# A conv and RWKV-7 block on one core: the last LayerNorm in the first phase, x loaded ahead in the second, BK times KR in quarters, squared keys summed in two products

## The chip, the cores and the metric

The kernel runs on one core of one Trainium2 chip. The core has TensorE (PE, matrix products, into the eight banks of PSUM), VectorE (DVE), ScalarE (ACT), GpSimd (POOL) and SyncE (SP); the last issues every DMA of this kernel, in the order in which they stand in its queue, and 16 DMA engines carry them between HBM and SBUF. The engines run each its own instruction stream and wait for each other on semaphores. The metric is device microseconds for one execution, less is better.

## The reference, cut to what matters

```python
D_MODEL = 1024; SEQ = 2048; CONV_WIDTH = 31; RWKV_HEAD = 64          # one batch, one layer
h = _rmsnorm(x, norm_g) * (1.0 + scale) + shift
p = h @ w_in                                                          # 1024 -> 9344
c_val, c_gate, c_og, ts, r_og, g_conv, g_rwkv = split(p)
# convolution branch
u = c_val * sigmoid(c_gate)
u = causal_depthwise_conv(u, conv_k, conv_b)                          # width 31
u = layernorm(u, ln_g, ln_b); y_conv = (silu(u) * silu(c_og)) @ w_conv_out
# RWKV-7 branch
r, k, v, w_low, a_low = split(token_shift(ts, mu))
decay = exp(-exp(-softplus(-(w0 + tanh(w_low) @ w2)) - 0.5)); a = sigmoid(a0 + a_low @ a2)
kk = k * k_k; kk = kk / max(sqrt(sum(kk * kk, per head)), 1e-12)
k = k * (1 + (a - 1) * k_a)
state = state * decay - (state @ kk) (kk * a)^T + v k^T;  o = state @ r   # a scan over time
o = layernorm(o, per head); o = (o + sum(r * k * r_k) * v) * silu(r_og); y_rwkv = o @ w_rwkv_out
# merge
m = sigmoid(g_conv) * y_conv + sigmoid(g_rwkv) * y_rwkv
out = _rmsnorm(x + gate * (m @ w_out), final_g)
```

All data are fp32.

## The kernel before

The 2048 positions are four blocks `b` of 512 (`TB`), the 1024 channels eight tiles of 128; features lie on partitions, time along the free axis. Each large product is made of three fp32r products: weights and activations are split into a rounded part `hi` and a remainder `lo` (an ACT cast and a DVE or POOL subtraction), and `mm3k` issues hi·hi, hi·lo and lo·hi into one PSUM bank. A projection of one weight tile is 24 such matmuls.

**First phase.** For each block, four groups `g` of four heads (two channel tiles, "pairs") are worked. The projections of `w_in` run all the time; between them stand, in bursts, the small products of the RWKV scan. `pair` prepares decay and keys of two heads: squared keys `sq` go through `bones` (a matrix of ones in two blocks of 64) to give each head's sum, which is copied (`ssr`) and sent by DMA (`dN`) to the place where the inversion of the group reads it; then BK times KR gives the 64 by 64 matrices within a chunk, two heads `hh` on the two halves of the rows. `group` inverts them (31 steps on POOL) and runs the chain over the eight chunks. `conv` makes u, and `taps` the 31 taps of its channel tile as 31 DVE operations; three u tiles exist. The result goes to `y_dram`. `lnorm_first(b)` is the LayerNorm of the conv branch for blocks 0 to 2, on POOL for the most part: it loads y three times (sum, squared differences, result), writes `u_dram`, and takes its tiles from a ring of seven, `hx`. The LayerNorm of block 3 is `lnorm(3)` in the second phase. `presplit` splits the output weights ahead of time and stores both parts.

After block 3, the output products `ro` and `co` of block 0 run (`rows0`).

**What sets the order.** The first phase is written by a planner. Generators (`Task`, by rank) yield conditions on planned times; `note` plans each instruction's time from a table of costs, and `poll` lets tasks issue while the projections go on matmul by matmul. `order` gives the sequence of projections in a group: three of k, r, v for each pair, and the fillings of the table `FILL`, for the last group `LAST` ("c" is a convolution, "1" to "4" the four gates). On the engines the order is then fixed. The second phase is ordered by the compiler's own scheduler.

**Second phase.** For each block: the conv output product (`cproj`, not for block 0), z and u of the next block loaded and split (`lsplit`), x loaded into `xt`, the output projection in four column blocks `cb` (PSUM tiles `pout`, 96 matmuls each), `addx` (adding x, and squares for the norm), `finish` (scale and store), then `rproj` for the next block, whose results `mr` use the buffers of `xt`. For block 0 `pout` uses the two banks that the projections use too. The program records nearly all instructions through one helper, so most lines of the profile read L129.

## Time and profile before

| | |
|---|---|
| median of 3 runs | 2893.17 us (2893.12 to 2894.62) |
| the profiled execution | 2892.82 us, its span 2890.7 us |
| mean granted TensorE clock | 0.982 |
| DMA | 680.47 MB, 235 GB/s, 69.0% of 16 engines' span |

The page cuts the span into 40 slices; a digit is the busy share of a slice in tenths:

```profile
PE   6999999889999999999999999999999998899998
DVE  6877787869677878885868787669787666543343
POOL 0564746533528355444656462648373633100000
DMA  8786767666757566776756686866666848676665
```

A slice is 72 us; the second phase begins in slice 34, at about 2397 us, where PE shows two 8s. In a row of groups, `out<-in` names the tiles, then come size and count, the busy time, the mean of one in ns, and after the second bar the idle time of the engine before them with what ended it. A matmul in fp32 leaves two records, one in fp32r leaves one; matmuls are pipelined, so a record's length is more than the time by which it holds the engine up, which is read from the distance of two starts.

### The profile page before, as it was taken

The numbers are of one execution on the slowest core, as the hardware profiler recorded it, in microseconds if no ns is written. First come the engines' busy times: TensorE is split into PE (matmuls) and PEld (weight loads), VectorE is DVE, ScalarE is ACT, GpSimd is POOL, SyncE is SP. The second block draws the span as 40 slices with busy tenths as digits, with TensorE's granted clock in tenths as the row PEclk, the third lists the DMA queues.
The fourth block names the chain that finished last, engine by engine and source line by source line (L and its number), as shares of the span: only waits on it lengthen the run. The fifth ranks groups of instructions, "written<-read, shape, count | busy, mean of one in ns | idle before, by whom it ended". The sixth has DMA issues, their size and how long they took to land.

```text
span 2890.7 us, 52304 instructions
## 1 busy us (share of the span) xinstructions
PE 2725.4 (94%) x19472; PEld 2201.6 (76%) x19472; DVE 2058.8 (71%) x3575; ACT 1090.7 (38%) x2180; POOL 1257.7 (44%) x1772
## 2 busy tenths in 40 slices
PE   6999999889999999999999999999999998899998
PEld 5777777667777777787777777777777777698988
DVE  6877787869677878885868787669787666543343
ACT  5545344434243434443434443333434233221211
POOL 0564746533528355444656462648373633100000
PEclk9999999989999999999999999999999999999999
DMA  8786767666757566776756686866666848676665
GB/s 329 255 295 219 281 221 263 237 227 234 231 187 257 183 218 237 250 258 221 252 181 233 205 294 201 273 211 215 205 246 213 294 158 314 234 240 229 215 226 175
DMA packets 361742, 680.47 MB, mean 235 GB/s; under 512 B 134160, under 2 KB 152912, under 8 KB 361488
## 3 DMA queue, kind: packets, MB, share of 16 engines
q1 hardware_dynamic: 361488, 677.13, 69.0%
q8 instruction: 154, 2.52, 0.4%
q14 instruction: 100, 0.82, 0.1%
HBM read 494.34 MB, written 181.54 MB: 234 GB/s over the span
## 4 chain that ended last, share of the span: by engine, by line
PE 32%; DVE 9%; POOL 7%; DMA 5%; issue 3%; ACT 1%; SPq 1%; DVEq 0%; POOLq 0%; ACTq 0%
PE ps_main L129 21%; PE pout L129 5%; DVE acc L129 3%; PE xo L129 2%; PE aux L129 2%; POOL TT L129 2%; POOL itmp L129 1%; PE late L129 1%; SPq L129 1%; DVE S L129 1%; DMA w_lo<-kl_in 1%; POOL oc L129 1%; DVE gst L129 1%; DVE rs_t L129 1%; POOL lny L129 1%
## 5 line engine op out<-in xcount | busy, mean ns | idle before, releaser
L129 PE MATMUL ps_main<-h_hi,w_hi 128*128 128x512 f32 x2432 | 1016.7, 418 | 17.4 <-DVE lora L129 4.6
L129 PE MATMUL ps_main<-h_hi,w_lo 128*128 128x512 f32 x2432 | 967.7, 398 | 20.3 <-POOL w_lo L129 13.6
L129 PE MATMUL ps_main<-h_lo,w_hi 128*128 128x512 f32 x2432 | 963.8, 396 | 2.0 <-DVE h_lo L129 2.0
L129 DVE SCALAR_TENSOR_TENSOR acc<-u,ck,acc 128x512 f32<-128x512 f32 x928 | 697.5, 752 | 25.3
L129 PEld LDWEIGHTS ps_main<-h_hi,w_lo 128*128 128x128 f32 x2432 | 463.4, 191 | 130.7 <-POOL w_lo L129 16.8
L129 PEld LDWEIGHTS ps_main<-h_hi,w_hi 128*128 128x128 f32 x2432 | 464.0, 191 | 128.9 <-issue 10.0
L129 PEld LDWEIGHTS ps_main<-h_lo,w_hi 128*128 128x128 f32 x2432 | 464.9, 191 | 99.8 <-issue 7.8
L129 POOL TENSOR_TENSOR w_lo<-w_st,w_hi 128x1024 fp32r<-128x1024 f32 (+1 forms) x83 | 165.2, 1990 | 302.9 <-ACT w_hi L129 248.7
L129 POOL TENSOR_TENSOR TT<-TT,itmp 128x126 f32<-128x126 f32 (+22 forms) x496 | 207.3, 418 | 38.9
L129 ACT ACTIVATE th<-ps_main 128x512 f32<-128x512 f32 x160 | 95.6, 598 | 333.9 <-PE ps_main L129 281.7
L129 ACT CAST w_hi<-w_st 128x1024 fp32r<-128x1024 f32 (+1 forms) x135 | 127.2, 943 | 243.2 <-DMA w_st<-w_co_t 137.3
L129 POOL TENSOR_TENSOR itmp<-La,TT 128x126 f32<-128x126 f32 (+22 forms) x496 | 200.8, 405 | 37.1 <-issue 6.4
L129 DVE SCALAR_TENSOR_TENSOR S<-xo,pe,Se 64x64 f32<-64x64 f32 x512 | 145.0, 283 | 90.1 <-PE xo L129 65.3
L129 ACT COPY uv<-xo 64x256 f32<-64x256 f32 (+1 forms) x192 | 81.0, 438 | 238.3 <-PE xo L129 164.7
L129 POOL TENSOR_TENSOR lny<-lny 128x512 f32<-128x512 f32 x90 | 119.9, 1340 | 108.9 <-DMA lny<-y_d 87.0
L129 DVE TENSOR_TENSOR w_lo<-w_st,w_hi 128x1024 fp32r<-128x1024 f32 x52 | 72.4, 1392 | 68.3 <-PE ps_main L129 46.5
L129 ACT ACTIVATE Se<-S,pe 128x128 f32<-128x128 f32 x256 | 88.7, 396 | 83.2 <-DVE S L129 82.7
L129 DVE TENSOR_TENSOR As<-aux,maskA 128x512 f32<-128x512 f32 x128 | 82.3, 685 | 52.5 <-PE aux L129 52.5
L129 POOL TENSOR_TENSOR wlo<-wf,wl 64x128 fp32r<-64x128 f32 x64 | 31.2, 488 | 149.6 <-ACT wl L129 147.0
L129 ACT ACTIVATE t<-ps_main,mu 128x512 f32<-128x512 f32 x96 | 65.9, 687 | 77.6 <-PE ps_main L129 68.0
L129 DVE TENSOR_TENSOR xt<-pout,xt 128x256 f32<-128x256 f32 x64 | 24.4, 419 | 99.3 <-PE pout L129 93.2
L129 PEld LDWEIGHTS xo<-S,KR 128*128 128x128 f32 x512 | 76.8, 189 | 23.9 <-DVE S L129 5.3
(298 smaller groups left out, 5029.0 us busy)
## 6 DMA issues: line engine op xcount, KB each, us to landing
w_hi<-kh_in SPq DMA_DIRECT2D x219, 512.0 KB
w_lo<-kl_in SPq DMA_DIRECT2D x219, 512.0 KB
w_st<-w_in_t SPq DMA_DIRECT2D x73, 512.0 KB
kh_in<-w_hi SPq DMA_DIRECT2D x71, 512.0 KB
kl_in<-w_lo SPq DMA_DIRECT2D x71, 512.0 KB
lny<-y_d SPq DMA_DIRECT2D x72, 256.0 KB
w_hi<-kh_ro SPq DMA_DIRECT2D x32, 512.0 KB
w_lo<-kl_ro SPq DMA_DIRECT2D x32, 512.0 KB
```

The lines of the kernel that those rows point to most:

```text
L129: r = f(*a, **k)
```

## The change

Four things change together.

1. `pair`: `sq` is split into `sq_hi` and `sq_lo`, and two fp32r products with `bones` take the place of one in fp32.
2. `pair`: each product of BK and KR is cut into two column halves of BK; in turn come the two heads' first halves, then their second.
3. `lnorm_first` serves all four blocks. The second pass writes y minus mean back to `y_dram`, the square goes to a tile of its own, and the third pass no longer subtracts. For the last block it runs on DVE, as a task of its own that starts when all convolutions are done, on tiles lent to it (`more`). The convolutions of block 3 come earlier (`LAST` now has a row for each group), block 2's LayerNorm moves from the second to the first group of block 3, and presplits leave block 3 for blocks 1 and 2. `lnorm` goes, with its pools.
4. Second phase: x is loaded before z, u is loaded after the output projection's code, `final_g` later, and eight instead of six tiles hold such loads (`LDB`).

```diff
+LDB = 8
+SLACK = 2.0
-LAST = ("c", "1", "c", "3", "4", "2", "1", "3", "4", "2")
+LAST = ("c0 10 20 c1 21 11 22 c2 23", "c3 12 24 c4 25 13 26 c5 27", "c6 14 30 c7 31 15 32 33 34 35",
+        "16 36 37 40 41 17 42 43 44 45 46 47")
...
+    class Slots(Ring):
...
# pair
-        yield burst(ok(sq), free, bank("aux"))
+        yield ok(sq)
+        sh = e1.tile([P, TB], F32R, name="sq_hi", tag=RHT)
+        nc.scalar.copy(sh, sq)
+        yield ok(sh)
+        sl = e1.tile([P, TB], F32R, name="sq_lo", tag=YT)
+        dve = max(now[0], vt["POOL"]) > max(now[0], vt["DVE"]) + W2
+        (nc.vector if dve else nc.gpsimd).tensor_tensor(out=sl, in0=sq, in1=sh.bitcast(F32), op=ALU.subtract)
+        yield burst(ok(sl), free, bank("aux"))
         pss = pa.tile([P, TB], F32, name="aux", tag="aux")
-        nc.tensor.matmul(pss, bones.bitcast(F32), sq, start=True, stop=True)
+        nc.tensor.matmul(pss, bones, sh, start=True, stop=False)
+        nc.tensor.matmul(pss, bones, sl, start=False, stop=True)
...
-                for hh in range(2):
+                for i in range(4):
+                    hh, half = i % 2, i // 2
                     hs = slice(64 * hh, 64 * hh + 64)
-                    nc.tensor.matmul(pA[hh][:, c // 2, es], BK[hs, cc, es], KR[hs, cc, es],
-                                     start=(c == 0), stop=(c == 3), skip_group_check=True)
+                    rs = slice(64 * half, 64 * half + 64)
+                    nc.tensor.matmul(pA[hh][rs, c // 2, es], BK[hs, cc, e * 128 + 64 * half:e * 128 + 64 * half + 64],
+                                     KR[hs, cc, es], start=(c == 0), stop=(c == 3), skip_group_check=True)
...
# lnorm_first
+        eng = nc.vector if b + 1 == NB else nc.gpsimd
...
-            nc.gpsimd.tensor_tensor(out=yj, in0=yj, in1=mean, op=ALU.subtract)
-            yield ok(yj)
-            nc.scalar.activation(yj, yj, AF.Square)
+            eng.tensor_tensor(out=yj, in0=yj, in1=mean, op=ALU.subtract)
+            yield both(ok(yj), hx.room(1))
+            yq = hx.take("lnq")
+            nc.scalar.activation(yq, yj, AF.Square)
+            nc.sync.dma_start(y_dram[b][j], yj)
+            hx.give(yj)
...
             yield ok(yj, rl)
-            nc.gpsimd.tensor_tensor(out=yj, in0=yj, in1=mean, op=ALU.subtract)
-            yield idle("POOL", 0.3)
-            nc.gpsimd.tensor_tensor(out=yj, in0=yj, in1=rl, op=ALU.mult)
+            eng.tensor_tensor(out=yj, in0=yj, in1=rl, op=ALU.mult)
...
# sides
-        if b and g == 1:
-            yield from lnorm_first(b - 1)
+        if b and g == (0 if b + 1 == NB else 1):
+            yield from lnorm_first(b - 1, hx)
+            if b + 1 == NB:
+                yield from lend(3)
         if b:
-            for _ in range((4, 2, 2, 0)[g] if b + 1 == NB else (1, 0, 1, 2)[g]):
+            for _ in range(0 if b + 1 == NB else (1, 1, 3, 3)[g]):
...
+    def last_norm():
+        yield when(lambda: len(convs) == KT * NB and convs[-1].done)
+        yield from lnorm_first(NB - 1, more)
...
# second phase
-    def lnorm(b):
...
-        if b + 1 < NB:
-            ohl = lsplit(z_dram[b + 1], okt(b + 1))
-            uhl = lsplit(u_dram[b + 1], utiles()) if b + 2 < NB else lnorm(b + 1)
         xts = []
...
+        if b + 1 < NB:
+            ohl = lsplit(z_dram[b + 1], okt(b + 1))
+        if b == 0:
+            nc.sync.dma_start(fg, final_g.unsqueeze(0).broadcast_to([P, D]))
...
         if b + 1 < NB:
+            uhl = lsplit(u_dram[b + 1], utiles())
             rall = tail_rs(0, NTT)
```

The planner and the scheduler move instructions by this. Three places are shown, each first as it stands before and then after the change; the lines' own number changes from L129 to L132, since the helper moved.

On SP, at the head of the second phase, the loads around the first x tile (`zt` from `z_d` and `y` belong to the splits and the LayerNorm of before, `ct` is the gate c_og, `w_hi` and `w_lo` are weights of the output projection):

```order
L129 DMA zt<-z_d_4_79 128x512
L129 DMA zt<-z_d_5_80 128x512
L129 DMA rth<-gr_d_0_267 128x512
L129 DMA rth<-gr_d_1_268 128x512
L129 DMA y_27755<-y_d_6_193 128x512
L129 DMA y_27758<-y_d_7_194 128x512
L129 DMA ct<-co_d_0_219 128x512
L129 DMA ct<-co_d_1_220 128x512
L129 DMA xt_25415<-x_in 128x512
```
```order
L132 DMA w_lo<-kl_o_1_18191 128x1024
L132 DMA z_d_7_98<-oc 128x512
L132 DMA w_hi<-kh_o_0_18520 128x1024
L132 DMA zt<-z_d_0_75 128x512
L132 DMA zt<-z_d_1_76 128x512
L132 DMA zt<-z_d_2_77 128x512
L132 DMA xt_26206<-x_in 128x512
```

The x tile moved ahead of z tiles 3 to 7, of both gate tiles `rth` and of the y and c_og tiles, which are gone from here; behind the eight x tiles now come five z tiles, `final_g`, and `w_lo` of the third weight pair.

On DVE, at the end of block 0's output projection, from the sum of squares (`vs`) on (`rs` and `rs_t` are the reciprocal root, `y` and `th` the last LayerNorm):

```order
L129 TENSOR_REDUCE vs<-sq_25431 128x4
L129 TENSOR_SCALAR vs<-vs 128x4
L129 TENSOR_SCALAR rs_25907<-vs 128x4
L129 SCALAR_TENSOR_TENSOR y_27738<-th,y_27738 128x512
L129 TENSOR_TENSOR rs_t<-rs_25907 128x4
L129 TENSOR_TENSOR y_27738<-y_27738,ct 128x512
L129 SCALAR_TENSOR_TENSOR rs_t<-rs_t,vs 128x4
```
```order
L132 TENSOR_REDUCE vs<-sq_26271 128x4
L132 TENSOR_SCALAR vs<-vs 128x4
L132 TENSOR_SCALAR rs_26781<-vs 128x4
L132 TENSOR_TENSOR rs_t<-rs_26781 128x4
L132 SCALAR_TENSOR_TENSOR rs_t<-rs_t,vs 128x4
L132 SCALAR_TENSOR_TENSOR rs_26781<-rs_t,rs_26781 128x4
```

The `y` operations between the steps of the root are gone, and so are those between the scaling of `xt` and the first `mr`.

On PE, in block 3, around the head sums of one pair (`xo` is the chain of another group):

```order
L129 MATMUL ps_main<-h_lo,w_hi 128x512
L129 MATMUL ps_main<-h_hi,w_lo 128x512
L129 MATMUL aux<-sq,bones 128x512
L129 MATMUL ps_main<-h_hi,w_hi 128x512
L129 MATMUL ps_main<-h_lo,w_hi 128x512
```
```order
L132 MATMUL xo<-uv,tk 64x64 x4
L132 MATMUL xo<-uv,As 64x64 x8
L132 MATMUL aux<-sq_hi,bones 128x512
L132 MATMUL aux<-sq_lo,bones 128x512
L132 MATMUL ps_main<-h_hi,w_hi 128x512
```

One product became two, back to back, and the projections around them shifted against the chain.

More of the change, by code (lines that the diff above doesn't have):

```diff
@@ L237, in give, with room, __init__, take @@
                 self.free.append(max(ready.get(key(t), 0.0), used.get(key(t), 0.0)))
+    class Slots(Ring):
+        def room(self, n=1, keep=0):
+            return Ring.room(self, n)
+        def __init__(self, slots):
+            self.free, self.slots, self.held = [0.0] * len(slots), list(slots), {}
+        def take(self, name):
+            self.free.remove(min(self.free))
+            slot = self.slots.pop(0)
+            t = slot(name)
+            self.held[key(t)] = slot
+            return t
+        def give(self, *ts):
+            Ring.give(self, *ts)
+            self.slots.extend(self.held.pop(key(t)) for t in ts)
     dbg = dbg or {}
@@ L1256, in lnorm_first @@
             hx.give(yj)
-        hx.give(mean, rl)
+        hx.give(rl)
     def lora_split(ps, out_):
@@ L1336, in sides, with slot_of @@
                     yield from presplit(*n_, half)
+    def slot_of(pool, tag, n):
+        return lambda name: pool.tile([P, TB], F32, name=name, tag=tag, bufs=n)
+    more = Slots([slot_of(e2, "u", 3)] * 3 + [slot_of(e2, "yj", 1)])
     reached, normed = [-1], [0]
@@ L1343, in side_work, with lend @@
             yield from sides(n // 4, n % 4)
+    def lend(n):
+        yield hx.room(n)
+        for _ in range(n):
+            more.free.append(min(hx.free))
+            hx.free.remove(min(hx.free))
+            more.slots.append(hx0)
+    def last_norm():
+        yield when(lambda: len(convs) == KT * NB and convs[-1].done)
+        yield from lnorm_first(NB - 1, more)
     def proj(h, ti, name, box):
@@ L1484, in hybrid_block @@
               enumerate(("M", "ta", "E2", "k", "r", "vv", "y", "sh"))]
+        more.free.extend([0.0] * 3)
+        more.slots.extend(slot_of(e1, t_, 1) for t_ in ("lw", "la", "E1"))
         h = rows0(h, "ro", gr_dram[0], u_dram[0])
@@ L1507, in ldt @@
     def ldt(name, src):
-        t_ = ob.tile([P, TB], F32, name=name, tag="ld", bufs=6)
+        t_ = ob.tile([P, TB], F32, name=name, tag="ld", bufs=LDB)
         nc.sync.dma_start(t_, src)
@@ L1557, in hybrid_block @@
     fg = f2.tile([P, D], F32, name="fg", tag="fg", bufs=1)
-    nc.sync.dma_start(fg, final_g.unsqueeze(0).broadcast_to([P, D]))
-    def t2(name):
-        return b2.tile([P, TB], F32, name=name, tag="t2", bufs=3)
     def utiles():
```

84 lines of the change are left out of this document (33 added, 51 removed).

## The prediction

> **What bounds the kernel now.** The page's table of busy time comes first, then the same by stage.
>
> ```profile
> PE 2725.4 (94%) x19472; PEld 2201.6 (76%) x19472; DVE 2058.8 (71%) x3575; ACT 1090.7 (38%) x2180; POOL 1257.7 (44%) x1772
> ```
> ```profile
> 2180.00:2340.00 160.00, 153.65 (x1298) 121.56 (x1297) 111.62 (x191) 49.97 (x101) 67.60 (x101) 0.97 0.78 261
> 2340.00:2397.00 57.00, 54.01 (x333) 42.93 (x332) 40.22 (x72) 17.89 (x34) 21.34 (x10) 1.00 0.41 130
> 2566.00:2625.00 59.00, 57.65 (x434) 55.13 (x434) 26.31 (x57) 17.61 (x49) 0.00 (x0) 1.00 0.74 255
> 2397.30:2412.70 15.40, 12.26 (x97) 11.29 (x95) 11.64 (x12) 5.43 (x10) 10.56 (x7) 1.00 1.04 393
> 2397.30:2487.00 89.70, 63.22 (x438) 57.83 (x437) 70.02 (x100) 40.68 (x87) 36.58 (x24) 0.90 0.87 314
> ```
>
> The second view gives, for each stretch, its length, then the busy time of TensorE (PE), its weight loads, VectorE (DVE), ScalarE (ACT) and GpSimd (POOL), the granted clock, the DMA share and GB/s. TensorE is busy for 2725.4 of 2890.7 us, so the time falls either by less TensorE work or by less of the 165.3 us in which it is idle. The idle time is not even. The stretch 2397.3 to 2487 opens the second phase: the output projection of block 0 and the first two tiles of the next RWKV projection. It takes 89.7 us and leaves TensorE idle for 26.5 of them, at a clock of 0.90. The same work one block later, 2566 to 2625, takes 59.0 us (434 records against 438, four of which are the LayerNorm's column sums). The waits of the long stretch name the cause:
>
> ```profile
> PE ps_main L129 <- DVE mr L129: 12.8, 1, 12.8
> PE pmean L129 <- POOL ys L129: 6.3, 1, 6.3
> PE pout L129 <- DVE o_lo L129: 2.6, 3, 1.1
> PE pout L129 <- DVE xt L129: 2.5, 1, 2.5
> PE pout L129 <- DMA w_lo<-kl_o: 1.8, 1, 1.8
> ```
>
> Columns: total us, times, longest. The 6.3 us is TensorE standing at a matmul of `lnorm(3)` whose sum GpSimd has not finished, and the 12.8 us is a PSUM bank that VectorE frees late. VectorE's own order of time shows why:
>
> ```profile
> 2419.02 0.42 DVE L129 TENSOR_TENSOR xt<-pout,xt 128x256 f32<-128x256 f32 x1 [3.43 <-DMA xt<-x_in]
> 2478.29 5.39 DVE L129 SCALAR_TENSOR_TENSOR xt<-xt,rs,fg 128x512 f32<-128x512 f32 x8
> 2483.59 1.89 DVE L129 SCALAR_TENSOR_TENSOR y<-th,y 128x512 f32<-128x512 f32 x3
> 2486.00 1.28 DVE L129 SCALAR_TENSOR_TENSOR mr<-rth,ps_main 128x512 f32<-128x512 f32 x2
> ```
>
> The x tiles land only at 2419, behind z, y and c_og tiles in SP's queue. Without them the output projection cannot leave PSUM. Later the LayerNorm's `y` operations stand between the block's end and `mr`.
>
> **The change part by part.** *The head sums of squared keys.* Now one fp32 product, afterwards two fp32r products:
>
> ```profile
> 82.57 0.39 PE L129 MATMUL ps_main<-h_hi,w_lo 128*128 128x512 f32 x1
> 82.80 1.02 PE L129 MATMUL aux<-sq,bones 128*128 128x512 f32 x2
> 83.26 0.79 PE L129 MATMUL ps_main<-h_hi,w_hi 128*128 128x512 f32 x1
> 83.89 0.39 PE L129 MATMUL ps_main<-h_lo,w_hi 128*128 128x512 f32 x1
> ```
>
> An fp32r product occupies 0.23 us (82.57 to 82.80). The fp32 one holds TensorE from 82.80 until one such step before 83.89, that is 83.66: 0.86 us. Two fp32r products take 0.46, so a pair saves 0.40 us and 32 pairs save 12.8 us. Added are one ACT cast and one subtraction for each pair, half of them on DVE and half on POOL, in a chain that TensorE already waits for:
>
> ```profile
> PE aux L129 <- ACT sq L129: 13.4, 12, 2.6
> L129 PE MATMUL aux<-rh,bones 128*128 128x512 f32 x32 | 16.3, 509 | 5.2 <-ACT tk L129 3.8
> L129 ACT CAST rh<-rk 128x512 fp32r<-128x512 f32 x32 | 19.8, 620 | 49.2 <-DVE rk L129 49.1
> L129 POOL TENSOR_TENSOR s_lo<-rk,rh 128x512 fp32r<-128x512 f32 x32 | 46.4, 1450 | 23.2 <-ACT rh L129 19.7 <-DVE uv L129 3.3
> ```
>
> The kernel has the same form already: `rk` is cast (0.62 us), subtracted (1.45 us) and multiplied by `bones` in two products, and TensorE loses 5.2 us in all before them. So the wait could fall from 13.4 to about 5 (8 less). If nothing covered the longer chain it would grow by 2.07 us in each of 32 pairs (66 more). The planner knows both new steps and puts projections ahead of the product, as it does for `rk`, but here no other matmul of the pair lies between; I leave the 13.4 as it is. What hides the chain is the projection work, and what is late if it fails is `ssr`, then the copies to `dN`, which the inversion needs.
>
> *BK times KR in quarters.* 8 matmuls of 64 rows by 128 columns become 16 of 64 by 64, over the same 128 moving columns. A burst now, and a burst that already runs in quarters:
>
> ```profile
> 93.73 0.40 PE L129 MATMUL ps_main<-h_hi,w_lo 128*128 128x512 f32 x1
> 94.05 1.16 PE L129 MATMUL aux<-KR,BK 64*128 64x128 f32 x16
> 95.14 0.50 PE L129 MATMUL ps_main<-h_hi,w_hi 128*128 128x512 f32 x1
> ```
> ```profile
> 219.67 0.40 PE L129 MATMUL ps_main<-h_hi,w_lo 128*128 128x512 f32 x1
> 220.00 0.27 PE L129 MATMUL late<-As,Tn 64*64 64x64 f32 x1
> 220.94 0.22 PE L129 MATMUL late<-As,Tn 64*64 64x64 f32 x1
> 221.09 0.60 PE L129 MATMUL xo<-S,KR 128*128 128x128 f32 x3
> ```
>
> The first costs 95.14 - 93.73 - 0.23 = 1.18 us for 16 records of 128 columns, two at a time. The second, whose first and last record are shown, has 64 records of 64 columns, four at a time, and costs 221.09 - 219.67 - 0.23 = 1.19 us. The new burst has 32 records of 128 columns, the same 4096 columns as the second, so 1.19 us: no change over the 64 bursts. Bounds: if all four quarters ran at once and each took half as long, the 0.85 us of streaming (1.18 without about 0.33 at its ends) would halve, 64 x 0.43 = 27 us less; if only two ran at a time it would double, 64 x 0.85 = 54 us more. I take zero, since the second fence is the nearest row.
>
> *The last LayerNorm and the head of the second phase.* Gone from 2397 to 2487 are two column sums, the `y` operations and their waits; the x loads stand before five of the eight z loads. What remains there is the work of 2566 to 2625, hence 59.0 us, and the waits of the beginning that stay: 2.6 for `o_lo`, which splits `mr` as before, and one that I expect in a new place: `w_lo` of the third weight pair now stands behind 8 x, 5 z tiles and `final_g`. SP issues such tiles at the pace of this row, and the DMA engines, full, move 393 GB/s at the start of the stretch (its row above):
>
> ```profile
> 2413.57 5.02 SPq L129 DMA_DIRECT2D xt<-x_in  x8
> ```
>
> 0.63 us each, so the 17 issues ahead take 10.7 us. Issue starts where the last co projection frees a weight slot, about 2398; at 393 GB/s the 5.8 MB that are then under way (16 tiles of 256 KB, `final_g` and two weight halves of 512 KB) need 14.7 us, so the tile lands between 2413 and 2416. TensorE wants it after the first quarter of the `pout` work (59.0 less 48 products of 0.23 us is 48, a quarter 12) and 2.6 of waits, at 2412. I charge 4 us, the later end. Sum: 59 + 2.6 + 4 = 65.6 instead of 89.7, a gain of 24 us; between 31 (59 us exactly) and 12 (the weight wait and half of the `mr` wait stay).
>
> *What the first phase takes on.* The last LayerNorm runs on DVE: 38 sums and products, 8 of the swish and 11 for the root, 57 operations at the 0.67 us of the `xt` row above (5.39 for 8), or 38 us, and the eight convolutions of block 3 are in hand by its third group.
>
> ```profile
> L129 DVE SCALAR_TENSOR_TENSOR acc<-u,ck,acc 128x512 f32<-128x512 f32 x928 | 697.5, 752 | 25.3
> 1725.00:1880.00 155.00, 148.85 (x1082) 118.97 (x1081) 111.86 (x189) 60.34 (x124) 74.45 (x112) 0.99 0.73 243
> L129 POOL TENSOR_TENSOR lny<-lny 128x512 f32<-128x512 f32 x90 | 119.9, 1340 | 108.9 <-DMA lny<-y_d 87.0
> ```
>
> One more convolution in a group is 31 x 0.752 = 23 us, which brings DVE's 111.9 us of 155 in block 3's first group to 135; it fits, but each evacuation then queues more often behind a tap. In the last group two convolutions (47 us) leave and the 38 us come, so DVE's 111.6 us of 160 hardly moves. GpSimd loses 24 subtractions of 1.34 us (32 us) and gains 16 key subtractions. DMA carries 64 more tiles, 16.8 MB; some 12.6 MB of them fall between 2180 and 2397, which at 390 GB/s is 32 us of queue, where the shares 0.78 and 0.41 leave 69 us free. The eight weight presplits that leave block 3 make room as well. Bounds: nothing, and 15.5 us if the added queueing doubles TensorE's idle time in the three rows concerned (6.2 in the first group, 6.3 and 3.0 from 2180 on). I charge 6, nearer to the lower end, since every added load fits its stretch.
>
> Sum against the profiled span: 2890.7 - 12.8 + 0 - 24 + 6 = 2859.9. The runs' median lies 2.5 us above the span (2893.17), hence **2862 us**.
>
> **The rivals.** (1) *Quarters run two at a time.* For it: two quarters of the same 64 rows read the same KR columns. Against it: the `As,Tn` burst, which also meets all four corners. Price 54 us, hence 2916, slower; the change comes out slower from 31 us, that is 0.48 us more in each burst. (2) *Quarters halve the burst.* For it is only that four corners are used instead of two. Against it: as long as the moving columns stay 64, records last alike for 128 by 64 and 64 by 64:
>
> ```profile
> L129 PE MATMUL xo<-uv,As 128*64 128x64 f32 x1024 | 40.8, 222 | 0.0
> L129 PE MATMUL xo<-uv,As 64*64 64x64 f32 x1024 | 35.3, 220 | 0.2 <-issue 0.2
> ```
>
> A column half is thus no faster than the whole, and its count doubles. It would give 2862 - 27 = 2835. The Trainium skill, TensorEngine Tiling (Array Packing), section Theoretical Speedup, allows up to twice the speed for each dimension of 64 or less; by it alone the burst would halve. The two rows above do not bear that out for the stationary columns. (3) *Block 3 gives it back*: DVE and DMA, fuller there, cost 22 us instead of 6, somewhat beyond the doubled idle time: 2878. For it: the first group's 135 us of 155. Against it: GpSimd and the presplits make room. (4) *The second phase stays DMA-bound.* The output projection's weights, x, z, u and the prefetched next z are some 17 MB, 43 us at 393 GB/s, nearly as long as the 48 us of `pout`; with the 12 us end of the bound the time is 2874. (5) *Nothing on balance*, (3) and (4) together: about 2890.
>
> **How the numbers follow.** Likeliest case 0.55 (its own range 2850 to 2872), rival (1) 0.06, (2) 0.04, (3) 0.17, (4) 0.12, (5) 0.06. The range 2843 to 2885 leaves out (1), (2), part of (5) and the edges. For this kernel 0.2% (6 us) is what a measurement tells from no change. Faster: 0.55 + 0.04 + 0.17 + 0.12 = 0.88. Case (5) is split over no change, 0.04, and slower, 0.02, to which (1) adds 0.06: 0.08.
>
> **What would show it.** The stretch from the first `pout` to the first waiting `ps_main` of the next projection should take about 66 us, with no `pmean` and a wait for `mr` under 4 us. `sq_hi` and `sq_lo` should stand 0.23 us apart, with waits before them of 5 to 20 us in all. A quarter burst should take 1.1 to 1.3 us between projections; 2 us would make (1) right, 0.8 us (2). TensorE should be busy some 14 us less up to the second phase. If its idle time before `pout` grows by more than 15 us over now, with VectorE or weight DMAs as releasers in block 3, (3) was right.

## The result, and the profile after

The changed kernel takes 2900.86 us (median of 20 runs, 2889.93 to 2915.04), the kernel before 2893.31 us in 20 runs beside it: a ratio of 1.0026, 95% interval 1.0015 to 1.0037. It is slower by 0.26%, where 2862 us were predicted. The profiled execution has a span of 2896.4 us at a granted clock of 0.981. Single slow executions of p1, p4 and p12 below (3.7 to 13.5 ms) are left out of their ratios.

The page's row of busy time, and the same by stage, cut at the first `pout` (2397.3 us before, 2426.6 us after); the columns of the second view are as in the prediction.

```profile
PE 2715.6 (94%) x20496; PEld 2193.8 (76%) x20496; DVE 2073.7 (72%) x3613; ACT 1111.9 (38%) x2213; POOL 1223.0 (42%) x1742
```

Before:

```profile
0.00:2397.30 2397.30, 2270.46 (x16781) 1797.41 (x16782) 1833.21 (x3182) 972.06 (x1925) 1221.13 (x1748) 0.98 0.70 236
2397.30:2565.80 168.50, 142.02 (x773) 122.81 (x772) 102.50 (x142) 53.74 (x102) 36.58 (x24) 0.93 0.77 266
```

After:

```profile
0.00:2426.60 2426.60, 2267.98 (x17808) 1793.64 (x17808) 1887.63 (x3256) 1009.52 (x1983) 1223.03 (x1742) 0.98 0.71 241
2426.60:2570.00 143.40, 134.64 (x768) 118.72 (x769) 63.27 (x107) 37.76 (x78) 0.00 (x0) 0.98 0.79 284
2426.60:2492.30 65.70, 58.40 (x432) 55.57 (x432) 34.22 (x70) 24.98 (x63) 0.00 (x0) 0.95 0.95 347
```

The second phase did what was forecast. From the first `pout` of block 0 to that of block 1 it takes 143.4 us instead of 168.5, a gain of 25. The third row of the view after is the head, cut just behind the last of its 432 records. The term of 24 was reckoned to the end of the wait for `mr`: by that measure the head takes 67.2 us (2426.6 to 2493.8) where the sum said 65.6 and before took 89.4, a gain of 22. All of the miss lies ahead of it. The first phase was to end 6.8 us earlier (12.8 less, 6 more) and ends 29.3 us later. TensorE's busy time there falls by 2.5 us, where some 14 were forecast, and its idle time grows from 126.8 to 158.6 us (length less busy time). Of the 31.8 us of new idle time, 16.9 lie ahead of block 3 (its first projection starts at 1755.4 us, before at 1743.8) and 14.9 in it. The waits of TensorE (total us, times, longest):

```profile
PE aux L132 <- POOL KR L132: 26.1, 14, 4.4
PE ps_main L132 <- POOL w_lo L132: 16.5, 8, 3.8
PE aux L132 <- DVE As L132: 13.3, 19, 2.7
...
PE aux L132 <- DVE sq_lo L132: 7.4, 8, 1.4
...
PE ps_main L132 <- DVE mr L132: 5.3, 3, 2.4
...
PE aux L132 <- POOL sq_lo L132: 4.5, 6, 1.1
PE pout L132 <- DVE xt L132: 4.4, 1, 4.4
```

Before, `KR` stood at 10.2 us and `As` at 4.7. The wait at the squared keys is what it was: 7.4 and 4.5 for `sq_lo` with 1.6 for `sq_hi` make 13.5, against 13.4. The growth is spread over many waits, `KR` (15.9 more) and `As` (8.6 more) ahead. Two groups of the changed kernel show the new matmuls:

```profile
L132 PE MATMUL aux<-KR,BK 64*64 64x128 f32 x2048 | 80.3, 290 | 36.1 <-POOL KR L132 26.1 <-DVE As L132 9.8
L132 PE MATMUL aux<-sq_lo,bones 128*128 128x512 f32 x32 | 14.6, 457 | 12.1 <-DVE sq_lo L132 7.4 <-POOL sq_lo L132 4.5
L132 PE MATMUL aux<-sq_hi,bones 128*128 128x512 f32 x32 | 13.4, 417 | 1.6 <-ACT sq_hi L132 1.6
```

The bursts of quarters took 80.3 us of records and 36.1 us of waiting, after 78.2 and 15.2. So the first theory, A, was that cast and subtraction stand in the pair's own sequence, so that everything after the square comes later, `KR` last. The rivals: B, the planner's cost of a quarter (0.117 us each, 1.88 us for a burst that the prediction put at 1.19) drives plan and chip apart; C, what costs time is that the order of the first phase is another one, whatever makes it so; D, the last group of block 3 cannot take the LayerNorm.

### The profile page after: what moved, and what is told of

Its sections match the earlier page's. It is cut to its first block, busy times and chain, and to the rows that moved or that the text cites. A ratio compares the mean times of both kernels' runs of the same rounds, so it can differ in the third digit from the quotient of the medians.

```text
span 2896.4 us, 54470 instructions
## 1 busy us (share of the span) xinstructions
PE 2715.6 (94%) x20496; PEld 2193.8 (76%) x20496; DVE 2073.7 (72%) x3613; ACT 1111.9 (38%) x2213; POOL 1223.0 (42%) x1742
## 5 line engine op out<-in xcount | busy, mean ns | idle before, releaser
L132 PE MATMUL ps_main<-h_hi,w_hi 128*128 128x512 f32 x2432 | 1006.4, 414 | 19.2 <-DMA w_hi<-kh_in 4.9
L132 PE MATMUL ps_main<-h_hi,w_lo 128*128 128x512 f32 x2432 | 967.1, 398 | 23.4 <-POOL w_lo L132 16.5
L132 PE MATMUL ps_main<-h_lo,w_hi 128*128 128x512 f32 x2432 | 963.1, 396 | 2.5 <-DVE h_lo L132 2.5
L132 DVE SCALAR_TENSOR_TENSOR acc<-u,ck,acc 128x512 f32<-128x512 f32 x928 | 697.8, 752 | 28.7 <-POOL u L132 4.0
L132 PEld LDWEIGHTS ps_main<-h_hi,w_lo 128*128 128x128 f32 x2432 | 463.0, 190 | 137.8 <-POOL w_lo L132 20.6
L132 PEld LDWEIGHTS ps_main<-h_hi,w_hi 128*128 128x128 f32 x2432 | 464.3, 191 | 124.6 <-issue 17.5
L132 PEld LDWEIGHTS ps_main<-h_lo,w_hi 128*128 128x128 f32 x2432 | 464.8, 191 | 94.0 <-DVE h_lo L132 4.5
L132 POOL TENSOR_TENSOR w_lo<-w_st,w_hi 128x1024 fp32r<-128x1024 f32 (+1 forms) x83 | 166.7, 2009 | 338.6 <-ACT w_hi L132 318.3
L132 POOL TENSOR_TENSOR TT<-TT,itmp 128x126 f32<-128x126 f32 (+22 forms) x496 | 212.9, 429 | 38.9
L132 POOL TENSOR_TENSOR itmp<-La,TT 128x126 f32<-128x126 f32 (+22 forms) x496 | 207.9, 419 | 37.8 <-issue 6.3
L132 DVE SCALAR_TENSOR_TENSOR S<-xo,pe,Se 64x64 f32<-64x64 f32 x512 | 145.1, 283 | 103.7 <-PE xo L132 68.1
L132 ACT ACTIVATE th<-ps_main 128x512 f32<-128x512 f32 x160 | 95.6, 597 | 320.1 <-PE ps_main L132 287.5
L132 ACT CAST w_hi<-w_st 128x1024 fp32r<-128x1024 f32 (+1 forms) x135 | 127.4, 944 | 232.6 <-DMA w_st<-w_co_t 146.5
L132 ACT COPY uv<-xo 64x256 f32<-64x256 f32 (+1 forms) x192 | 81.2, 439 | 244.8 <-PE xo L132 178.0
L132 DVE TENSOR_TENSOR w_lo<-w_st,w_hi 128x1024 fp32r<-128x1024 f32 x52 | 73.9, 1422 | 66.7 <-PE ps_main L132 51.9
L132 ACT ACTIVATE Se<-S,pe 128x128 f32<-128x128 f32 x256 | 88.9, 396 | 68.8 <-DVE S L132 68.4
L132 PE MATMUL aux<-KR,BK 64*64 64x128 f32 x2048 | 80.3, 290 | 36.1 <-POOL KR L132 26.1
L132 DVE TENSOR_TENSOR As<-aux,maskA 128x512 f32<-128x512 f32 x128 | 82.4, 685 | 42.9 <-PE aux L132 42.4
L132 PEld LDWEIGHTS aux<-KR,BK 64*64 64x64 f32 x2048 | 62.0, 141 | 60.1 <-POOL KR L132 35.7
L132 PEld LDWEIGHTS xo<-S,KR 128*128 128x128 f32 x512 | 77.2, 190 | 27.0 <-ACT Se L132 8.5
L132 PE MATMUL xo<-S,KR 128*128 128x128 f32 x512 | 89.0, 290 | 8.3 <-DVE S L132 7.0
L132 DVE TENSOR_TENSOR xt<-pout,xt 128x256 f32<-128x256 f32 x64 | 24.4, 420 | 101.0 <-PE pout L132 101.0
```

Of the source, the lines that this page charges most:

```text
L132: r = f(*a, **k)
```

## The experiments

Eighteen kernels ran. "Idle" is TensorE's: the profiled span less the busy time. The first `pout` parts the phases; a wait of that `pout` itself counts as first phase. The ratio is to the runs of before that were taken beside each version (their medians lie from 2890.0 to 2893.3 us), so it is not always the quotient of two rows. Busy, idle and the phases come from one profiled execution, which can lie some 10 us off the median (p3's lies 8 above it, p8's 13 above, p10's 6 below).

| run | median us | ratio to before (95%) | busy | idle | first pout | from there |
|---|---|---|---|---|---|---|
| before | 2893.3 | 1 | 2725.4 | 165.3 | 2397.3 | 493.4 |
| changed | 2900.9 | 1.0026 (1.0015, 1.0037) | 2715.6 | 180.8 | 2426.6 | 469.8 |
| p1 split only | 2912.7 | 1.0060 (1.0037, 1.0083) | 2716.9 | 190.5 | 2419.4 | 488.0 |
| p2 quarters only | 2917.4 | 1.0081 (1.0057, 1.0106) | 2730.1 | 185.4 | 2427.6 | 487.9 |
| p3 LayerNorm only | 2890.5 | 0.9998 (0.9980, 1.0017) | 2727.6 | 169.4 | 2419.5 | 477.5 |
| p4 sums aside | 2919.0 | 1.0087 (1.0058, 1.0115) | 2720.3 | 196.9 | 2453.5 | 463.7 |
| p5 quarters, old order | 2889.6 | 1.0008 (0.9993, 1.0022) | 2726.3 | 165.1 | 2396.1 | 495.3 |
| p6 quarters, true cost | 2898.6 | 1.0029 (1.0009, 1.0048) | 2716.3 | 178.1 | 2406.1 | 488.3 |
| p7 other order | 2895.7 | 1.0024 (1.0006, 1.0041) | 2715.3 | 181.2 | 2409.5 | 487.0 |
| p8 quarters, half cost | 2900.6 | 1.0053 (1.0034, 1.0071) | 2721.6 | 189.7 | 2429.3 | 482.0 |
| p9 x first only | 2891.0 | 0.9997 (0.9975, 1.0019) | 2723.8 | 167.8 | 2399.1 | 492.5 |
| p10 all, whole cost | 2905.9 | 1.0046 (1.0024, 1.0069) | 2715.8 | 182.1 | 2420.1 | 477.8 |
| p11 all, single square | 2926.5 | 1.0119 (1.0075, 1.0162) | 2725.2 | 201.0 | 2441.4 | 484.8 |
| p12 all, other order | 2888.7 | 0.9988 (0.9968, 1.0008) | 2706.3 | 179.7 | 2412.2 | 473.8 |
| p13 split, old order | 2918.7 | 1.0104 (1.0079, 1.0129) | 2729.9 | 187.0 | 2423.1 | 493.8 |
| p14 before, third order | 2897.7 | 1.0024 (1.0010, 1.0037) | 2722.3 | 173.3 | 2405.6 | 490.0 |
| p15 all, third order | 2903.6 | 1.0047 (1.0029, 1.0065) | 2716.3 | 184.5 | 2421.6 | 479.2 |
| p16 all, fourth order | 2917.2 | 1.0089 (1.0069, 1.0108) | 2723.9 | 192.7 | 2434.2 | 482.4 |
| p17 LayerNorm, block 3 | 2904.4 | 1.0050 (1.0033, 1.0067) | 2726.0 | 173.3 | 2435.8 | 463.5 |
| p18 all, chosen order | 2917.0 | 1.0089 (1.0070, 1.0109) | 2717.2 | 197.4 | 2437.2 | 477.4 |

**The parts alone (p1, p2, p3).** Each takes its piece of the diff above and leaves the others out.

> The kernel before with the split of the squared keys alone. Theory A (the chain behind the split: the cast and the subtraction stand between the square and everything that the pair issues after it, so that GpSimd's KR comes some 3 us later in each of 32 pairs and TensorE stands at the burst BK times KR): the wait aux<-POOL KR rises from 10.2 to about 25 us, the time from the square to the end of GpSimd's KR from 11.8 to about 14.6 us, TensorE's busy time falls by 7 to 13 us, and the kernel takes 2893 to 2903 us. Theory B (the table of planned times counts a quarter at 0.117 us, 1.88 us a burst, where the burst takes 1.18): without quarters the wait stays near 10 us and the kernel takes about 2881 us. Theory C (any other plan of the first phase moves it by some 10 us either way): the time moves without the KR wait explaining it.

> The kernel before with the quarters alone. Theory A: the burst stays at 0.8 to 0.9 us from first to last start, the KR wait stays near 10 us, and the kernel takes 2890 to 2896 us. Theory B (planned times drift from the chip's): 5 to 15 us slower than before, 2898 to 2908 us, with the KR wait up. Theory C: a change of several us either way, with the idle time spread over many waits.

> The changed kernel with the squared keys as one fp32 product and with whole BK times KR products: what is left is the last LayerNorm in the first phase and the second phase that loads x first. Theory A: the second phase gains 24 to 25 us (first pout of block 0 to first pout of block 1 143 to 145 us where it was 168.5), the first phase takes on at most 6 us, so 2870 to 2876 us. Theory D (the last group of the first phase gives most of it back, since the LayerNorm's loads and its VectorE work collide with the weights there: 17 of the 29 us lost lie there): the first phase is 15 to 20 us longer and the kernel takes 2883 to 2890 us.

The split alone costs 21 us, the quarters alone 26, the LayerNorm nothing that can be told. Their sum, about 45 us, is six times the 7.5 us of the whole: the parts do not add. In the split's kernel the KR wait is as A says, though the time lies 10 us above A's band:

```profile
PE aux L129 <- POOL KR L129: 27.2, 14, 6.7
```

But the quarters, which leave the pair's sequence as it was, cost more still, and A has nothing to say on that. The LayerNorm alone gains 15.9 us behind the first `pout` and arrives there 22.2 us later; 18 of these 22 are lost from block 3's first projection on (671.6 us from there to `pout`, before 653.4).

**Quarters and split in the order of before (p5, p13).** In p5 the table of planned times gives four quarters just the times of two whole products, so the planner writes the first phase in the order of before, row for row on every engine:

```diff
+                if quarter:
+                    c = N_ / 600 * quarter[0]
...
+                    quarter[:] = [(0.89, 0.0, 0.0, 0.89)[i]]
```

> The kernel before with the quarters, and with planned times that give the four quarters together and their last writes just the times of the two whole products: in the first phase every engine's instructions stand in the order of before, with sixteen quarters for eight products. What is left is what the quarters cost on the chip. If the 25 us of the quarters alone come from the plan (theories B and C): 2889 to 2896 us, bursts of 0.83 us. If they come from the chip (TensorE is slower with them, or the waits behind them grow): 2905 to 2918 us.

The first phase of p5, then its group of quarters:

```profile
0.00:2396.10 2396.10, 2268.50 (x17805) 1787.70 (x17806) 1837.33 (x3182) 971.53 (x1925) 1219.83 (x1748) 0.99 0.70 236
```
```profile
L132 PE MATMUL aux<-KR,BK 64*64 64x128 f32 x2048 | 75.9, 278 | 12.0 <-POOL KR L132 6.3 <-DVE As L132 5.6
```

Quarters cost nothing on the chip: 2396.1 us to the first `pout`, 12.0 us of waiting where before had 15.2. Between two projections, without a wait and at full clock, a burst takes 1.13 us (median of 38), before 1.19. The 26 us of p2 are the price of its order alone.

In p13 cast and subtraction are issued behind the planner's back, and the two products where the one stood:

```diff
+        sh = e1.tile([P, TB], F32R, name="sq_hi", tag=RHT)
+        tc.nc.scalar.copy(sh, sq)
+        sl = e1.tile([P, TB], F32R, name="sq_lo", tag=YT)
+        tc.nc.vector.tensor_tensor(out=sl, in0=sq, in1=sh.bitcast(F32), op=ALU.subtract)
         yield burst(ok(sq), free, bank("aux"))
         pss = pa.tile([P, TB], F32, name="aux", tag="aux")
-        nc.tensor.matmul(pss, bones.bitcast(F32), sq, start=True, stop=True)
+        tc.nc.tensor.matmul(pss, bones, sh, start=True, stop=False)
+        tc.nc.tensor.matmul(pss, bones, sl, start=False, stop=True)
+        note("PE", "matmul", pss, [bones.bitcast(F32), sq])
```

> The kernel before with the split of the squared keys, and a planner that does not know of it: it plans the one fp32 product, so that the first phase keeps the order of before; cast and subtraction (on VectorE) stand right behind the square and KR, the two products where the one stood. My own step, tested alone: TensorE's busy time falls by 12.8 us, and the wait that stood on ACT sq (13.4 us) now ends on sq_lo. If projections cover the longer chain there, that wait stays near 13 us and the kernel takes 2877 to 2884 us. If nothing does (cast 0.62 and subtraction 0.66 to 1.45 us in each of 32 pairs), the wait grows by 35 to 60 us and the kernel takes 2905 to 2940 us: the split then needs another order to pay at all, and the order is what has a price.

Its waits, and one of its 32 places:

```profile
PE aux L812 <- ACT sq_hi L807: 24.6, 23, 3.4
PE aux L813 <- DVE sq_lo L809: 15.5, 27, 1.8
```
```profile
81.79 0.39 PE L812 MATMUL aux<-sq_hi,bones 128*128 128x512 f32 x1
83.41 0.50 PE L813 MATMUL aux<-sq_lo,bones 128*128 128x512 f32 x1 [1.23 <-DVE sq_lo L809]
83.75 0.39 PE L129 MATMUL ps_main<-h_hi,w_hi 128*128 128x512 f32 x1
```

The wait goes from 13.4 to 40.1 us, which is as much as the loss (26.7 of 28 us). The saving is gone too, since a product that has been waited for costs more. Measured as in the prediction (from the projection ahead to the second one behind, less two steps of 0.23 and the waits, at full clock), the product of before holds TensorE for 0.86 us where nothing waits (median of 13 places) and for 1.13 where TensorE waits ahead of it (7 places). The two products of p13 hold it for 0.73 us at the place shown, with one wait, but for 1.01 at most places (median of 18), where it waits at both; and busy time does not fall (2729.9 after 2725.4). In the changed kernel, where a projection lies ahead and both halves are ready, the saving is what was forecast:

```profile
85.63 0.39 PE L132 MATMUL ps_main<-h_hi,w_lo 128*128 128x512 f32 x1
85.86 0.40 PE L132 MATMUL aux<-sq_hi,bones 128*128 128x512 f32 x1
86.10 0.40 PE L132 MATMUL aux<-sq_lo,bones 128*128 128x512 f32 x1
86.33 0.40 PE L132 MATMUL ps_main<-h_hi,w_hi 128*128 128x512 f32 x1
```

0.70 us from the projection ahead to the one behind, less its own 0.23, are 0.47 for the pair. At the changed kernel's places with one wait the two products hold TensorE for 0.74 us (median of 12), after 1.13: 0.39 us are saved either way. So the split pays in an order that gives it room, and loses 28 us in the order of before.

**What another order costs (p6, p7, p8, p14).** p7 and p14 change one constant of the kernel before, `SEM`, the planned time of a semaphore, from 0.10 to 0.11 and 0.09 us. p6 and p8 are p2 with a quarter planned at 0.074 and 0.095 us.

> The kernel before with nothing changed but one constant of the planner, the planned time of a semaphore, 0.11 us in place of 0.10: the same instructions, in another order from the first projections on. Theory C: 5 to 25 us slower than before, 2897 to 2915 us, as if it were one of the changes. Theories A and B: no change beyond a few us, 2888 to 2897 us.

> The kernel before with the planned time of a semaphore at 0.09 us: a third draw of its order. Theory C: TensorE idle for 140 us or more in the first phase and 2895 to 2915 us. If the planned times are merely better at one value than at another (a slope): on the other side of before from the 0.11 run, 2880 to 2890 us.

> The kernel before with the quarters, each planned at 0.074 us, so that a burst is planned at 1.18 us as the trace has it, where the old plan had 1.52 and the changed kernel's 1.88. Theory B (a plan that is nearer the chip is the better): at or below before, 2880 to 2893 us. Theory C (what counts is that the plan is another than the tuned one): 2897 to 2915 us although the planned times are nearer the measured ones.

> The kernel before with the quarters, each planned at half of a whole product, so that a burst is planned at 1.52 us as before; only the first bank's last write is planned 0.09 us later, and from there the order differs. Theory C: slower than before by 5 to 25 us, 2897 to 2915 us. Theory B: as before, 2889 to 2896 us, since the planned burst is as long as before's.

The same instructions in another order take 0.24% more, twice, with `SEM` to either side of 0.10: no slope. (p7's 2895.7 us lie in the band of A and B, below that of C, but 5.4 us above the runs of before beside it.) As to B, the planned burst is 1.18 us in p6, close to the chip's, and the kernel is still 8 us slower; with before's 1.52 it is 10 slower, with 1.88 it is 26. B may set the size, but not the sign: these four orders and that of p2 leave TensorE idle for 173 to 190 us. p7's first rows show where such time can land:

```profile
PE pout L129 <- ACT o_hi L129: 17.0, 1, 17.0
PE ps_main L129 <- DVE mr L129: 15.4, 2, 14.2
...
PE aux L129 <- POOL KR L129: 11.2, 13, 2.0
```

Here `KR` (11.2) is no worse than before, and one wait of 17 us stands between the phases, from a constant that touches neither.

**The whole change in other orders (p10, p12, p15, p16).** p10 plans the quarters as p5 does; p12, p15 and p16 set `SEM` to 0.11, 0.09 and 0.12.

> The whole change, with the quarters planned at the times of the two whole products, so that the planner lays the first phase out as if only the split and the LayerNorm were new. Theory C: another draw of the order; the head of the second phase keeps its gain (23 to 25 us less from the first pout to the end), the first phase takes 2408 to 2435 us, and the kernel 2880 to 2905 us. Theory B (the planned cost of the quarters is what hurts): 2870 to 2878 us.

> The whole change with the planned time of a semaphore at 0.11 us in place of 0.10 and nothing else: the same instructions in another order. Theory C: the time moves by 5 us or more either way, so between 2880 and 2920 us, by the idle time of the first phase; the head keeps its gain. Theories A and B: within 4 us of the changed kernel's 2901.

> The whole change with the planned time of a semaphore at 0.09 us. Theory C: a draw from the same spread as the changed kernel's others (2901, 2906, 2889), so 2885 to 2912 us, with the rest after the first pout at 455 to 470 us. A slope: past the changed kernel on the other side of the 0.11 run, 2908 to 2918 us.

> The whole change with the planned time of a semaphore at 0.12 us. Theory C: 2885 to 2912 us, no nearer to the 0.11 run (2889) than to the others. A slope: 2874 to 2884 us, past the 0.11 run.

2905.9, 2888.7, 2903.6 and 2917.2 us: one constant moves the same work by 28.5 us, and not in one direction (0.09, 0.10, 0.11, 0.12 give 2904, 2901, 2889, 2917). p16 left the expected band upwards, p10 by 1 us. Nor does the time from the first `pout` keep its gain as expected: p10 gains 15.6 us there, and p15 takes 479.2.

**The chain behind the squared keys (p4, p11).** p4 puts the head sums into a task of their own and `sq_lo` into another buffer; p11 is the changed kernel with the single product.

```diff
+        def head_sums():
...
+        sums = Task(head_sums(), 2)
...
+        yield when(lambda: sums.done)
         rh = e1.tile([P, TB], F32R, name="rh", tag=RHT)
```

> The changed kernel, with cast, subtraction, the two products and the copy of the head sums in a task of their own, so that y, BK and KR are issued without waiting for them; sq_lo takes the buffer of M in place of that of y. Theory A: the KR wait falls from 26 to 10 us or less (below before's, since before too waited for the fp32 product there), the time from the square to the end of KR falls below 12 us, and the kernel takes 2870 to 2882 us. Theory B or D: the KR wait may fall, but the time stays within 5 us of 2900.

> The changed kernel with the squared keys' head sums as one fp32 product again. Theory A (the chain behind the split cost the first phase its gain): the KR wait falls from 26 to 10 to 15 us and the kernel takes 2872 to 2885 us. Theory C: 2885 to 2915 us, with TensorE idle for 143 us or more in the first phase, as in every plan but that of before.

```profile
PE ps_main L132 <- POOL w_lo L132: 20.3, 10, 3.8
PE aux L132 <- DVE sq_lo L132: 17.2, 9, 4.3
PE late L132 <- DVE Tn L132: 16.2, 9, 4.2
...
PE aux L132 <- ACT sq_hi L132: 9.0, 4, 7.4
PE pout L132 <- ACT o_hi L132: 8.7, 1, 8.7
PE aux L132 <- POOL KR L132: 8.4, 11, 1.9
```

p4's waits: `KR` falls from 26.1 to 8.4 us, as A said, and the time rises by 18 us: TensorE now stands at `sq_lo`, `sq_hi`, `w_lo` and `Tn`. p11, which has no chain at all, is 26 us slower than the changed kernel. Both times lie above every band on record for them. So A's mechanism is real, and it has a price in a held order (p13), but where it was taken away nothing was gained. Both kernels are new orders too, so they do not show how much of the changed kernel's loss is A's.

**The two halves of the LayerNorm's part (p9, p17).** p9 loads x first in the kernel before, and leaves the last LayerNorm in the second phase.

> The kernel before with the second phase's part alone: x loaded ahead of z, the gain vector and u behind them, seven load buffers in place of six. The last LayerNorm stays in the second phase, and the first phase keeps the plan of before, instruction by instruction. If what cost the changed kernel its gain is the other order of the first phase, that phase takes 2397 us within 4 here. The wait for x at the head (2.5 us) and part of the late PSUM bank (12.8 us) go, the wait for the LayerNorm's sum (6.3 us) moves or stays: 5 to 15 us faster than before, 2876 to 2886 us. If the gain of the head comes from the LayerNorm's absence alone: 2887 to 2893 us.

```profile
PE ps_main L129 <- DVE mr L129: 11.2, 2, 9.8
PE pmean L129 <- POOL ys L129: 4.3, 1, 4.3
...
PE pout L129 <- DVE xt L129: 0.9, 1, 0.9
```

The wait for x falls from 2.5 to 0.9 us, the late bank only from 12.8 to 9.8, and the time from the first `pout` by 0.9 us: the head's gain is the LayerNorm's absence. p17 keeps before's order up to block 3; from there on it is the changed kernel without split and quarters, but with block 3's presplits left where they were.

```diff
+            yield from lnorm_first(b - 1, hx) if b + 1 == NB else lnorm_old(b - 1)
...
+            for _ in range((4, 2, 2, 0)[g] if b + 1 == NB else (1, 0, 1, 2)[g]):
...
+        if b + 1 == NB and g == 2:
+            yield from lend(3)
```

> The last LayerNorm in the first phase and the second phase as changed, but without split and quarters, and with the LayerNorms of blocks 0 and 1 and the presplits of blocks 1 and 2 as before, so that the order of the first phase is that of before up to the start of block 3 and differs only from there. Theory C (what is lost is lost wherever the order is new): up to the last block the times agree with before's within 4 us; the head keeps its gain of 16 to 24 us, block 3 takes on 5 to 15 us, and the kernel takes 2876 to 2888 us, faster than both. Theory D (block 3 itself cannot take the LayerNorm, more so as it keeps its eight presplits): the loss stands between the start of block 3 and the first pout, 18 us or more, and the kernel takes 2888 to 2900 us.

Up to block 3 the times agree (its first projection, the 220th, starts at 1747.5 us, before at 1743.8), and far into it too: the 233rd at 1855.3 against 1853.7, the 281st at 2215.2 against 2221.8. Then the end of block 3 loses more than the head gains:

```profile
2300.00:2350.00 50.00, 42.97 (x348) 33.12 (x350) 23.31 (x34) 9.28 (x14) 12.57 (x18) 0.86 0.76 265
2350.00:2430.00 80.00, 57.53 (x464) 44.18 (x455) 65.32 (x107) 29.54 (x52) 23.11 (x11) 0.90 0.55 179
```

VectorE is busy for 65.3 of the last 80 us, TensorE for 57.5, and the first `pout` waits 16.6 us for `o_hi`. Here the loss stands where D puts it, and the time (2904.4 us) lies above the bands of both theories. But the kernel also lends the LayerNorm its tiles only behind the last presplit, so it starts late; how much of that is D's collision and how much the late start isn't told apart.

**A chosen order (p18).** The whole change with a quarter at 0.074 us, `SEM` 0.105 and `JOIN` 2.5.

> The whole change, nothing left out, with three constants of the planner changed: a quarter planned at 0.074 us (the measured burst of 1.18 us), a semaphore at 0.105, the joining of bursts at 2.5. Several settings were laid out, and this is the one whose order the planner itself ends first. Theory C (the change is worth its time once the order is as good as the tuned one of before): TensorE idle for 115 to 140 us in the first phase, the first pout at 2385 to 2412 us, the rest 458 to 468 us, and 2862 to 2885 us, faster than both. If an order's quality on the chip cannot be had from the planner: another draw from 2885 to 2912 us, with 143 us or more idle. If the split and the LayerNorm cost the first phase its time in any order (theories A and D): 2895 us or more.

```profile
PE ps_main L132 <- POOL w_lo L132: 17.7, 9, 4.0
...
PE xo L132 <- DVE uv L132: 14.8, 18, 3.0
...
PE aux L132 <- POOL KR L132: 13.2, 13, 3.0
...
PE pout L132 <- DVE xt L132: 10.0, 1, 10.0
```

A miss: 197.4 us idle, at many places: `w_lo`, the chain's `uv`, `KR` and the first x tile among them. The order that the planner ends first is among the worst on the chip, so in this one try it did not find a good one. No version was shown to beat before; the lowest, p12, is 0.12% below it with an interval across zero.

## Why the prediction was wrong, point by point

*The second phase*: right in size for the changed kernel (24 predicted, 22 measured to the end of the wait for `mr`, 25 up to block 1's first `pout`), and in cause: p9 shows that x alone brings nothing, and in the changed kernel no `pmean` is left and the wait for `mr` at the head is 2.4 us. The size is partly luck: the `w_lo` that I charged with 4 us costs 1.3, the 2.6 of `o_lo` are 1.4 of `o_hi` and `o_lo`, and x costs 4.4 that I did not charge. And half of it depends on the order. From the first `pout` of block 0 to that of block 1 the five other orders of before's work (p2, p6, p7, p8, p14) take 157 to 164 us, not 168.5, and the six orders of the changed kernel (the changed one, p10, p12, p15, p16, p18) 143 to 154: 161.7 and 149.3 on average, a gain of 12. In some of these the head waits for loads as rival (4) had it: for `xt` 13.2 us in p16 and 10.0 in p18, for `w_hi` 8.7 in p15; the changed kernel's row above has the DMA share at 0.95.

*The quarters*: right. Zero was taken, p5 measures 1.0008 (0.9993 to 1.0022). Rivals (1) and (2) fall with it: the burst of 1.13 us is neither 2 nor 0.8. The Trainium skill, TensorEngine Tiling (Array Packing), section Theoretical Speedup, allows up to twice the speed for a dimension of 64 or less; the prediction was wrong to take from it that the burst would halve. Cutting the columns in two also doubles the number of products, so the factor of two leaves the burst about where it was, and the trace agrees (1.13 us after 1.19).

*The split*: right. The price of a product came down by the 0.40 us of the sum (0.39 measured, with a wait and without), so some 12.5 of the 12.8 us are saved at the head sums themselves. TensorE's busy time up to `pout` still falls by only 2.5 us, so some 10 are lost elsewhere. About 7 of these are the clock's, by an estimate: after the first 30 us TensorE is busy at half clock for 82.2 us of the first phase, before for 68.6, and half of the difference is lost.

*The step that failed* is the +6 for what the first phase takes on, with its bounds "nothing, and 15.5 us if the added queueing doubles TensorE's idle time in the three rows concerned". It counted three stretches of block 3 and took the rest of the first phase as it was. With 12.8 us saved and the phase 29.3 us longer, the term should have been 42 us: 31.8 of them are idle time, more than half of it ahead of block 3, where nothing was charged. Behind it stands the sentence that the planner "puts projections ahead of the product". It did, and the wait stayed at 13.5 us, as "I leave the 13.4 as it is" had it. But I booked that cover as free. In before's order the chain costs 26.7 us (p13); to avoid that the planner lays the phase out anew, and each of the five other orders of before's work cost 5 to 26 us, against the runs beside it.

These five (quarters count as free by p5) average 181.5 us of idle time and 2902.0 us, against 165.3 and 2893.3 in the order of before. The six orders of the changed kernel average 186.2 us idle, 2715.9 us busy and 2905.5 us. So the change as such, order against order, saves 5.2 us of TensorE's busy time (2721.1 for the five), adds 4.7 us of idle time, and is worth nothing within a scatter of about 10 us from order to order. By stages, on average: block 3 is reached 9 us later (1759.5 us against 1750.6), from there to the first `pout` takes as long (665.8 against 665.1), and the head is 12 us shorter. Leaving before's order costs 9 to 12 us on average (2902.0 against the 2890.4 to 2893.3 that before took beside these runs), which is more than the whole loss of 7.5.

Rival (3), block 3 gives it back, is what p3 and p17 look like, but the orders of before that have no LayerNorm there take as long for block 3, so the two are not told apart. Rival (5) came nearest in time for another reason, and the likeliest rival, a new order, was not among them.

What stays open: how the 32 us of new idle time in the changed kernel's first phase divide between the split's chain, the LayerNorm and the order. The runs show that they do not add, and no run holds the order fixed with all three in it. Why before's order leaves only 165 us idle isn't known either.

## What to carry to other kernels

Where a planner writes the order, an edit that it can see is two edits: the instructions, and a new order of everything behind them. Price the second by moving a constant that means nothing, before the first is summed to a few us: here that alone cost 0.24% of before, and moved the changed kernel by 28.5 us. And test an edit with its planned times held to the old ones (p5, p13); that separates what the chip charges from what the new order does.

## What the runs showed of the hardware

After a long wait TensorE runs at half pace for some microseconds, so a wait costs more than itself. p4's timeline around its longest wait, then the row of the stretch from the end of that wait on, whose third figure from the end is the granted clock:

```profile
778.09 0.40 PE L132 MATMUL ps_main<-h_hi,w_lo 128*128 128x512 f32 x1
785.92 0.80 PE L132 MATMUL aux<-sq_hi,bones 128*128 128x512 f32 x1 [7.43 <-ACT sq_hi L132]
...
787.89 0.63 PE L132 MATMUL ps_main<-h_hi,w_hi 128*128 128x512 f32 x1
788.32 0.63 PE L132 MATMUL ps_main<-h_lo,w_hi 128*128 128x512 f32 x1
...
792.16 0.53 PE L132 MATMUL ps_main<-h_lo,w_hi 128*128 128x512 f32 x1
792.52 0.40 PE L132 MATMUL ps_main<-h_hi,w_lo 128*128 128x512 f32 x1
792.76 0.39 PE L132 MATMUL ps_main<-h_hi,w_hi 128*128 128x512 f32 x1
```
```profile
785.92:792.16 6.24, 5.66 (x12) 4.09 (x13) 2.88 (x3) 2.96 (x6) 6.00 (x7) 0.50 0.91 282
```

From 787.89 to 792.16 ten steps take 0.427 us each, at a granted clock of 0.50, then 0.23 to 0.24 again: about 2 us more on top of the 7.43. "Busy" time holds this loss, so part of what an order costs is hidden in that column.

In all twenty profiles the clock changes on a fixed grid of 3.41 us (counted from 20 us on). It falls to a half after 301 of the 302 stretches of that grid (those at full clock) in which TensorE's waits come to 2 us or more, after 100 of the 254 with 1.5 to 2 us, and after 41 of the 15647 with less. 33 of the 302 hold no single wait above 1.8 us, and the clock fell after each of them: several short waits in one stretch do it as well as a long one.

The Trainium skill, TensorE: Matmul & The Clock Gate, section What's actually happening, has the clock halved after an idle window of about 3.4 us and full again after as long a busy one. The length of the window agrees with the grid measured here. That about 2 us of waiting within it are enough it does not say; the count above decides.
